# Gate products in eighths around a layer norm's three small matmuls, and the low halves of one weight matrix on VectorE alone

## The chip, the core and the metric

The kernel runs on one core of a Trainium2 chip. A core has TensorE (matrix products, into PSUM), VectorE, ScalarE and GpSimd (work on tiles, each with its own in-order queue), and SyncE, which here issues most loads from memory. The metric is the device time of one execution in microseconds.

## What is computed

One decoder block over 512 tokens of width 1024, float32. The part that the change touches, cut from the reference:

```
u = a * sigmoid(b)                          # gated linear unit
u = causal depthwise conv of width 31 (u) + conv_b
u = silu(layer_norm(u, conv_ln_g, conv_ln_b))
y_conv = u @ w_pw2 + b_pw2
merged = sigmoid(g_attn) * y_attn + sigmoid(g_conv) * y_conv
m = merged @ w_out                          # then x += rms_norm(m); then the squared-ReLU MLP
# layer_norm: mu = mean(x); var = mean((x-mu)^2); (x-mu) * rsqrt(var + eps) * g + b
```

The gate logits g_attn and g_conv are columns of h @ w_in.

## The kernel before

Every large product is made of three in a reduced float32 form: an operand is split in a high half and a low half (the rest), and `mm3` (lines 87 to 91) issues high x high, high x low and low x high. A weight piece is 128 x 512: `wsplit` (line 102) loads it into one of six "raw" tiles from SyncE's queue, casts the high half on ScalarE (line 114) and subtracts on an engine of choice for the low half (line 115). High and low halves of ordinary pieces go into four rotating tiles each, so a cast waits until TensorE has done with the piece four before it.

Work is tiled by blocks of 128 channels over all 512 tokens; a block takes eight steps k of three products of 512 columns, two weight pieces of four steps each. Channels stand on the partitions. `gate_parts` (line 390) is a generator that makes one block of gate logits and yields after each k; `gate` runs it through. Gates 0 to 7 belong to the attention branch; gates 8 to 15 to the convolution branch (names gt8 to gt15 and pg8 to pg15 in the order of instructions, gt and pg in the trace, which leaves numbers out). A gate ends with a multiply on VectorE (line 397) and a sigmoid on ScalarE (line 398) into a tile gB.

The layer norm of the convolution's output has its channels on the partitions, so sums over channels are matmuls with a matrix of ones. There are three small ones: `mub` (the mean, line 581), `st_var` (the variance, line 595, four 128 x 128 weight tiles of squares against one column) and `rsb` (the reciprocal deviation spread over all partitions, line 605). Between mub and st_var stand subtraction of the mean (line 586), squares on ScalarE (588) and sums on GpSimd and VectorE (590 to 593). Between st_var and rsb stand var (598), a power on GpSimd (`rstd_of`, rln, line 148) and four small products with the identity on VectorE (dg, 604). `gates_conv(lo, hi)` runs whole gates: two between mub and st_var, one between st_var and rsb, five after it. After rsb come the norm's scaling and swish (609 to 615), which make the split operand swh and swl.

Then `w_pw2` is multiplied block by block (pyb, line 631; its pieces' low halves are made on GpSimd), each block's result is merged with the gates and the attention branch into m (633, 634) and split into mgh and mgl. In between `load_wout(k)` loads row block k of w_out, with its low half (wol) on VectorE for odd k and on GpSimd for even k. Then `project_out` (pm, line 662) multiplies by w_out.

The order on each engine is set when the program is built: a scheduler places instructions by program order, dependencies and its own estimate of when they are ready. Each engine then runs its list strictly in that order.

Of the kernel before, what the change touches and what calls it, by code (L numbers as in the profile page):

```python
# [23 lines left out]
KD = D // P  # L24
# [9 lines left out]
NC_ = C // P  # L34
# [17 lines left out]
BRIDGE = 4  # L52
SPLIT = 2 * P
TAIL = 2
LN0, LN1, LN2 = 0, 2, 3


@with_exitstack
def decoder_block(ctx: ExitStack, tc: tile.TileContext, a: dict, out: bass.AP):
    nc = tc.nc  # L60
    pe, act, dve, pool, sp = nc.tensor, nc.scalar, nc.vector, nc.gpsimd, nc.sync
# [25 lines left out]
    def mm3(o, lh, ll, rh, rl, first, last):  # L87

        pe.matmul(o, lhsT=lh, rhs=rh, start=first, stop=False)  # L89
        pe.matmul(o, lhsT=lh, rhs=rl, start=False, stop=False)  # L90
        return pe.matmul(o, lhsT=ll, rhs=rh, start=False, stop=last)  # L91
# [10 lines left out]
    def wsplit(src, name, sizes=(512, 512), dst=None, eng=None):  # L102

        parts, off = [], 0
        for p, n in enumerate(sizes):
            raw = rtile(f"{name}_{p}", n)
            sp.dma_start(raw, src[:, off:off + n])
            if dst is None:
                hi = stage.tile([P, 512], F32R, tag="whi", name=f"whi_{name}_{p}", bufs=NSPLIT)[:, :n]
                lo = stage.tile([P, 512], F32R, tag="wlo", name=f"wlo_{name}_{p}", bufs=NSPLIT)[:, :n]  # L110
            else:
                hi, lo = (d[:, off:off + n] for d in dst)
            e = eng or pool
            recent[act] = act.copy(hi, raw)  # L114
            recent[e] = e.tensor_tensor(lo, raw, f32(hi), ALU.subtract)  # L115
            parts.append((off, n, hi, lo))
            off += n

        def cols(c0, n):
            for o, m, hi, lo in parts:  # L120
                if o <= c0 and c0 + n <= o + m:
                    return hi[:, c0 - o:c0 - o + n], lo[:, c0 - o:c0 - o + n]
            raise ValueError(f"columns {c0}:{c0 + n} of {name} lie in two pieces")

        return cols

    def stat(name, n=1, tag="stat", bufs=8):
        return const.tile([P, n], F32, tag=tag, name=name, bufs=bufs)
# [31 lines left out]
    def hsl(x, k, sl):  # L160
        return hT[x][k // 4][:, k % 4, sl]
# [8 lines left out]
    def ps(name):  # L170
        return psum.tile([P, 512], F32, tag="ps", name=name, bufs=3)
# [4 lines left out]
    def tps(name):  # L176
        return psum.tile([P, 512], F32, tag="tp", name=name, bufs=1)
# [29 lines left out]
    with ExitStack() as s1:  # L207
        r1 = open_pool(s1, "r1")
        w0 = []
        for k in range(KD):  # L210
# [5 lines left out]
            hi, lo = (r1.tile([P, Z0], F32R, tag=f"w0{x}", name=f"w0{x}{k}", bufs=8) for x in "hl")  # L216
# [173 lines left out]
    def gate_parts(i, dst):  # L390
        w = wsplit(a["w_zm"][2 * NC_ + i], f"gt{i}")
        pg = ps(f"pg{i}")
        for k in range(KD):
            mm3(pg, *w(k * P, P), hsl(0, k, full), hsl(1, k, full), k == 0, k == KD - 1)
            if k < KD - 1:
                yield
        dve.tensor_tensor(dst, pg, rxs, ALU.mult)
        act.activation(dst, dst, AF.Sigmoid)

    def gate(i, dst):  # L400
        for _ in gate_parts(i, dst):
            pass
# [3 lines left out]
    with ExitStack() as s3:  # L406
# [89 lines left out]
        for n in range(NT * H):  # L496
            h, i = divmod(n, NT)
# [22 lines left out]
    def wtile(name, dt=F32):  # L520
        return r3.tile([P, 2, 512], dt, tag="w", name=name, bufs=14)
# [5 lines left out]
    mA, gB = [], []  # L527
    for i in range(NC_):
# [3 lines left out]
        else:  # L532
            for _ in g0:
                pass
            for pr in range(H // 2):
                hi, lo = wtile(f"ah{pr}", F32R), wtile(f"al{pr}", F32R)
# [15 lines left out]
    for i0 in range(0, NC_, 2):  # L552
        acc = [cvtile(f"cv{i0 + j}") for j in range(2)]
        co = [upool.tile([P, S + 32], F32, tag="u", name=f"c{i0 + j}", bufs=9)[:, :S] for j in range(2)]
        for tap in range(CW):
            for j in range(2):
                i = i0 + j
# [10 lines left out]
            elif i0 + j:  # L568
                (dve if i0 + j == NC_ - 1 else pool).tensor_tensor(csum, csum, co[j], ALU.add)

    def gates_conv(lo, hi):
        for i in range(lo, hi):
            if i % 2 == 0:
                gB.append(wtile(f"gB{i}"))
            gate(NC_ + i, gB[i // 2][:, i % 2, :])

    gates_conv(0, LN0)


    mub = cvtile("mub")  # L580
    pe.matmul(mub, lhsT=ones, rhs=csum, start=True, stop=True)
    gates_conv(LN0, LN1)
    st_var = tps("st_var")
    s2 = []
    for i in range(NC_):
# [7 lines left out]
    dve.tensor_tensor(s2[7], s2[3], s2[7], ALU.add)  # L593
    for t in range(NT):
        pe.matmul(st_var[:, t:t + 1], lhsT=s2[7][:, t * P:(t + 1) * P], rhs=ones[:, 0:1], start=True, stop=True)
    gates_conv(LN1, LN2)
    var = stat("var", NT)
    dve.tensor_scalar(var, st_var[:, 0:NT], 1.0 / C, EPS, ALU.mult, ALU.add)
    rs = rstd_of(var, "rln", NT)
# [2 lines left out]
    for t in range(NT):  # L602
        sl = slice(t * P, (t + 1) * P)
        dve.tensor_scalar(dg[:, sl], ident, rs[:, t:t + 1], None, ALU.mult)
    pe.matmul(rsb, lhsT=ones, rhs=dg, start=True, stop=True)
    gates_conv(LN2, NC_)
    sw = [[r3.tile([P, 4, S], F32R, tag="sw", name=f"sw{x}{g}", bufs=4) for g in range(2)] for x in "hl"]
    for i in range(NC_):
        dve.tensor_tensor(cs[i], cs[i], rsb, ALU.mult)
# [10 lines left out]
    def load_wout(k):  # L620
        hi, lo = (wtile if k < 6 else ratile)(f"woh{k}", F32R), (wtile if k < 6 else ratile)(f"wol{k}", F32R)
        wsplit(a["w_out"][k], f"wout{k}", dst=[x.rearrange("p a b -> p (a b)") for x in (hi, lo)],
               eng=dve if k % 2 else pool)
        wo.append((hi, lo))

    mg = [[hpool.tile([P, 4, S], F32R, tag="h", name=f"mg{x}{g}", bufs=4) for g in range(2)] for x in "hl"]
    for i in range(NC_):
        w = wsplit(a["w_pw2"][i], f"pw{i}")
        py = ps(f"pyb{i}")
        for k in range(NC_):  # L630
            mm3(py, *w(k * P, P), sw[0][k // 4][:, k % 4, :], sw[1][k // 4][:, k % 4, :], k == 0, k == NC_ - 1)
        m_ = stile(f"m{i}")
        dve.scalar_tensor_tensor(m_, py, bpw[:, i:i + 1], gB[i // 2][:, i % 2, :], ALU.add, ALU.mult)
        dve.tensor_tensor(m_, m_, mA[i], ALU.add)
        split_psum(mg[0][i // 4][:, i % 4, :], mg[1][i // 4][:, i % 4, :], m_)
        while len(wo) < min(KD, i + 2):
            load_wout(len(wo))


    while len(wo) < KD:  # L640
        load_wout(len(wo))
# [257 lines left out]
def build(arrays):  # L899
    import concourse.bacc as bacc  # L900

    nc = bacc.Bacc("TRN2", target_bir_lowering=False, num_devices=1, dynamic_dma_scratch_size=8192)
    args = {}
    for n, v in arrays.items():
        args[n] = nc.dram_tensor(f"in_{n}", v.shape, mybir.dt.from_np(v.dtype), kind="ExternalInput").ap()
    o = nc.dram_tensor("out_0", (S, D), F32, kind="ExternalOutput").ap()
    with tile.TileContext(nc) as tc:
        decoder_block(tc, args, o)
    return nc
# [9 lines left out]
```

## Time and profile before

| | us |
|---|---|
| median of 3 runs | 820.9 (820.53 to 821.85) |
| the profiled execution | 821.58 |
| its span | 819.8 |
| TensorE busy | 789.4 (96%) |
| VectorE busy | 631.7 (77%) |
| ScalarE busy | 419.7 (51%) |
| GpSimd busy | 215.6 (26%) |

Busy shares are means over stages with different limits. TensorE's matmuls are pipelined: a row of 0.39 us for a product of 512 columns contains a tail that overlaps the next, and what counts is the distance between starts. The granted clock is a share of TensorE's full 2.4 GHz, so 0.50 is 1.2 GHz. Times of rows are microseconds from the span's start.

### The profile page before, as it was taken

How to read it: one execution, taken by the hardware profiler on the slowest of the kernel's cores; microseconds unless marked ns; L12 is line 12 of the kernel's file. 1: busy time of each engine (PE TensorE's matmuls, PEld its weight loads, DVE VectorE, ACT ScalarE, POOL GpSimd, SP SyncE). 2: the span in 40 equal slices, each digit the busy share in tenths (PEclk: the TensorE clock that was granted, in tenths of full speed). 3: DMA queues.
4: the chain of work that ended last, by engine and by line, in shares of the span. 5: the costliest groups of instructions: out<-in, count | busy, mean ns of one | idle time of the engine just before them, and what ended most of it. 6: DMA issues, size and time to landing. Idle time of an engine off the chain costs nothing. (4 is left out here: it accounts for less than half of the span.)

```text
span 819.8 us, 11002 instructions
## 1 busy us (share of the span) xinstructions
PE 789.4 (96%) x3786; PEld 662.7 (81%) x3786; DVE 631.7 (77%) x1046; ACT 419.7 (51%) x792; POOL 215.6 (26%) x203
## 2 busy tenths in 40 slices
PE   8989999999999999899999999999999999999991
PEld 8977888888887888687877898888888888788881
DVE  5689999999999996587563538676766666798777
ACT  7566876876763323366442314444444344556642
POOL 4244334333534545647640110000000000000003
PEclk9999999999999999899999999999999999999996
DMA  8412121122112223235551014444433434565422
GB/s 269 137 42 91 52 81 53 45 88 71 65 65 90 97 97 113 93 134 171 172 191 39 17 36 154 142 167 142 162 133 129 155 128 146 179 214 204 167 69 102
DMA packets 54344, 96.36 MB, mean 118 GB/s; under 512 B 6288, under 2 KB 11280, under 8 KB 54288
## 3 DMA queue, kind: packets, MB, share of 16 engines
q1 hardware_dynamic: 53856, 94.09, 34.3%
q0 software_dynamic: 432, 1.57, 0.6%
q8 instruction: 30, 0.49, 0.3%
q14 instruction: 26, 0.21, 0.1%
HBM read 93.54 MB, written 2.10 MB: 117 GB/s over the span
## 5 line engine op out<-in xcount | busy, mean ns | idle before, releaser
L562 DVE SCALAR_TENSOR_TENSOR cv<-u,convw,cv 128x512 f32<-128x512 f32 x232 | 161.9, 747 | 0.2
L90 PE MATMUL pf<-h2l,whi_f 128*128 128x512 f32 (+1 forms) x256 | 96.2, 376 | 0.0
L89 PE MATMUL pf<-h2h,whi_f 128*128 128x512 f32 (+1 forms) x256 | 96.2, 376 | 0.0
L91 PE MATMUL pf<-h2h,wlo_f 128*128 128x512 f32 (+1 forms) x256 | 96.0, 376 | 0.0
L115 DVE TENSOR_TENSOR wlo_f<-raw_f,whi_f 128x512 fp32r<-128x512 f32 x60 | 41.1, 691 | 61.1 <-ACT whi_f L114 58.8
L852 POOL TENSOR_TENSOR e<-e,v 128x512 f32<-128x512 f32 x2 | 3.2, 1594 | 321.5 <-DVE e L849 321.5
L114 ACT CAST whi_f<-raw_f 128x512 fp32r<-128x512 f32 x60 | 36.9, 621 | 81.4 <-DMA raw_f<-in_w_ff 42.7
L115 POOL TENSOR_TENSOR wlo_gt<-raw_gt,whi_gt 128x512 fp32r<-128x512 f32 x32 | 43.9, 1373 | 50.5 <-ACT whi_gt L114 50.5
L89 PEld LDWEIGHTS pf<-h2h,whi_f 128*128 128x128 f32 x256 | 48.2, 188 | 8.8
L90 PEld LDWEIGHTS pf<-h2l,whi_f 128*128 128x128 f32 x256 | 48.2, 188 | 8.7
L91 PEld LDWEIGHTS pf<-h2h,wlo_f 128*128 128x128 f32 x256 | 48.2, 188 | 8.7
L89 PE MATMUL pg<-hTh,whi_gt 128*128 128x512 f32 x128 | 51.9, 405 | 0.0
L90 PE MATMUL pg<-hTl,whi_gt 128*128 128x512 f32 x128 | 50.8, 397 | 0.0
L91 PE MATMUL pg<-hTh,wlo_gt 128*128 128x512 f32 x128 | 50.7, 396 | 0.0
L89 PE MATMUL p<-yh,l 128*128 128x512 f32 x128 | 49.7, 390 | 0.0
L90 PE MATMUL p<-yl,l 128*128 128x512 f32 x128 | 49.7, 389 | 0.0
L91 PE MATMUL p<-yh,l 128*128 128x512 f32 x128 | 49.5, 389 | 0.0
L729 ACT CAST yh<-f 128x512 fp32r<-128x512 f32 x48 | 28.1, 619 | 32.8 <-PE p L90 25.2
L730 DVE TENSOR_TENSOR yl<-f,yh 128x512 fp32r<-128x512 f32 x48 | 31.7, 686 | 12.9 <-ACT yh L729 12.9
L114 ACT CAST whi_gt<-raw_gt 128x512 fp32r<-128x512 f32 x32 | 19.8, 618 | 41.3 <-PE pg L90 38.4
L729 ACT CAST xh<-t 128x512 fp32r<-128x512 f32 x48 | 29.8, 621 | 19.5 <-DVE t L754 19.5
L730 DVE TENSOR_TENSOR xl<-t,xh 128x512 fp32r<-128x512 f32 x48 | 31.6, 686 | 0.0
(314 smaller groups left out, 2279.8 us busy)
## 6 DMA issues: line engine op xcount, KB each, us to landing
f<-in_w_ff SPq DMA_DIRECT2D x128, 256.0 KB, 3.0
raw_f<-in_w_ff SPq DMA_DIRECT2D x64, 256.0 KB, 3.1
raw_gt<-in_w_zm SPq DMA_DIRECT2D x32, 256.0 KB, 2.5
raw_gb<-in_w_zm SPq DMA_DIRECT2D x16, 256.0 KB, 2.6
raw_ga<-in_w_zm SPq DMA_DIRECT2D x16, 256.0 KB, 2.6
raw_wo<-in_w_o SPq DMA_DIRECT2D x16, 256.0 KB, 2.6
raw_pw<-in_w_pw SPq DMA_DIRECT2D x16, 256.0 KB, 2.9
raw_wout<-in_w_out SPq DMA_DIRECT2D x16, 256.0 KB, 2.7
```

The costliest lines, as they stand in the source:

```text
L89: pe.matmul(o, lhsT=lh, rhs=rh, start=first, stop=False)
L90: pe.matmul(o, lhsT=lh, rhs=rl, start=False, stop=False)
L91: return pe.matmul(o, lhsT=ll, rhs=rh, start=False, stop=last)
L114: recent[act] = act.copy(hi, raw)
L115: recent[e] = e.tensor_tensor(lo, raw, f32(hi), ALU.subtract)
L562: dve.scalar_tensor_tensor(co[j] if tap == CW - 1 else acc[j], src, convw[:, i, tap:tap + 1], acc[j], ALU.mult, ALU.add)
L729: act.copy(hi, src)
L730: dve.tensor_tensor(lo, src, f32(hi), ALU.subtract)
L852: pool.tensor_tensor(e[:, t, :], e[:, t, :], v, ALU.add)
```

## The change

The three constants that named whole gates become two that count eighths of gates: 21 eighths between mub and st_var (gates 8 and 9 and five eighths of gate 10), five between st_var and rsb (the rest of gate 10 and two eighths of gate 11), the other 38 after rsb. The second call also moves in program order, from ahead of var to behind dg. And w_out's low halves are all made on VectorE.

```
-LN0, LN1, LN2 = 0, 2, 3
+LN1, LN2 = 21, 5
...
-    def gates_conv(lo, hi):
-        for i in range(lo, hi):
+    def gates_conv():
+        for i in range(NC_):
             if i % 2 == 0:
                 gB.append(wtile(f"gB{i}"))
-            gate(NC_ + i, gB[i // 2][:, i % 2, :])
-
-    gates_conv(0, LN0)
+            yield from gate_parts(NC_ + i, gB[i // 2][:, i % 2, :])
+            yield
+
+    gates = gates_conv()
+
+    def run_gates(n):
+
+        for _ in range(n):
+            next(gates, None)
 
 
     mub = cvtile("mub")
     pe.matmul(mub, lhsT=ones, rhs=csum, start=True, stop=True)
-    gates_conv(LN0, LN1)
+    run_gates(LN1)
     st_var = tps("st_var")
...
         pe.matmul(st_var[:, t:t + 1], lhsT=s2[7][:, t * P:(t + 1) * P], rhs=ones[:, 0:1], start=True, stop=True)
-    gates_conv(LN1, LN2)
     var = stat("var", NT)
...
         dve.tensor_scalar(dg[:, sl], ident, rs[:, t:t + 1], None, ALU.mult)
+    run_gates(LN2)
     pe.matmul(rsb, lhsT=ones, rhs=dg, start=True, stop=True)
-    gates_conv(LN2, NC_)
+    run_gates(NC_ * KD)
...
         wsplit(a["w_out"][k], f"wout{k}", dst=[x.rearrange("p a b -> p (a b)") for x in (hi, lo)],
-               eng=dve if k % 2 else pool)
+               eng=dve)
```

How instructions move, at three places. TensorE around st_var, before (pg9 is gate 9's accumulator, pg10 gate 10's):

```order
L90 MATMUL pg9_3602<-hTl1_103,whi_gt9_1_3598 128x512
L91 MATMUL pg9_3602<-hTh1_101,wlo_gt9_1_3599 128x512
L595 MATMUL st_var_3629<-ones_86,s27_3656 128x1 x4
L89 MATMUL pg10_3678<-hTh0_100,whi_gt10_0_3668 128x512
L90 MATMUL pg10_3678<-hTl0_102,whi_gt10_0_3668 128x512
```

and now:

```order
L91 MATMUL pg10_3642<-hTh0_100,wlo_gt10_0_3633 128x512
L89 MATMUL pg10_3642<-hTh1_101,whi_gt10_1_3638 128x512
L90 MATMUL pg10_3642<-hTl1_103,whi_gt10_1_3638 128x512
L91 MATMUL pg10_3642<-hTh1_101,wlo_gt10_1_3639 128x512
L601 MATMUL st_var_3658<-ones_86,s27_3685 128x1 x4
L89 MATMUL pg10_3642<-hTh1_101,whi_gt10_1_3638 128x512
L90 MATMUL pg10_3642<-hTl1_103,whi_gt10_1_3638 128x512
```

Five eighths of gate 10 have moved ahead of st_var.

GpSimd around the power rln, before (wlo_gt11_1 is the low half of gate 11's second weight piece):

```order
L115 TENSOR_TENSOR wlo_gt11_0_3719<-raw_gt11_0_3716,whi_gt11_0_3718 128x512
L115 TENSOR_TENSOR wlo_gt11_1_3725<-raw_gt11_1_3722,whi_gt11_1_3724 128x512
L148 TENSOR_TENSOR rln_3707<-var_3705,mhalf_87 128x4
L115 TENSOR_TENSOR wlo_gt12_0_3759<-raw_gt12_0_3756,whi_gt12_0_3758 128x512
L115 TENSOR_TENSOR wlo_gt12_1_3765<-raw_gt12_1_3762,whi_gt12_1_3764 128x512
```

and now:

```order
L115 TENSOR_TENSOR wlo_gt11_0_3718<-raw_gt11_0_3715,whi_gt11_0_3717 128x512
L115 TENSOR_TENSOR wlo_gt11_1_3724<-raw_gt11_1_3721,whi_gt11_1_3723 128x512
L115 TENSOR_TENSOR wlo_gt12_0_3759<-raw_gt12_0_3756,whi_gt12_0_3758 128x512
L148 TENSOR_TENSOR rln_3696<-var_3694,mhalf_87 128x4
L115 TENSOR_TENSOR wlo_gt12_1_3765<-raw_gt12_1_3762,whi_gt12_1_3764 128x512
```

The power has moved behind the low half of gate 12's first piece.

VectorE at the beginning of the pointwise products, before (swl1 is the last channel's low half; wol1 a low half of w_out's second row block; m0 the first merged block):

```order
L615 TENSOR_TENSOR swl1_3916<-si7_3967,swh1_3914 128x512
L397 TENSOR_TENSOR gB6_3834<-pg14_3847,rxs_266 128x512
L115 TENSOR_TENSOR wol1_4030<-raw_wout1_0_4031,woh1_4029 128x512
L115 TENSOR_TENSOR wol1_4030<-raw_wout1_1_4035,woh1_4029 128x512
L397 TENSOR_TENSOR gB6_3834<-pg15_3886,rxs_266 128x512
L633 SCALAR_TENSOR_TENSOR m0_4014<-pyb0_3989,vecs_90,gB0_3550 128x512
```

and now:

```order
L621 TENSOR_TENSOR swl1_3916<-si7_3967,swh1_3914 128x512
L115 TENSOR_TENSOR wol0_4020<-raw_wout0_0_4021,woh0_4019 128x512
L115 TENSOR_TENSOR wol0_4020<-raw_wout0_1_4025,woh0_4019 128x512
L115 TENSOR_TENSOR wol1_4030<-raw_wout1_0_4031,woh1_4029 128x512
L115 TENSOR_TENSOR wol1_4030<-raw_wout1_1_4035,woh1_4029 128x512
L397 TENSOR_TENSOR gB6_3834<-pg15_3886,rxs_266 128x512
L115 TENSOR_TENSOR wol2_4082<-raw_wout2_0_4083,woh2_4081 128x512
L115 TENSOR_TENSOR wol2_4082<-raw_wout2_1_4087,woh2_4081 128x512
L639 SCALAR_TENSOR_TENSOR m0_4014<-pyb0_3989,vecs_90,gB0_3550 128x512
```

Four low halves have been added ahead of m0, and gate 14's multiply now stands ahead of swl1.

## Rows read from the trace of the kernel before

**Rows 1.** TensorE's waits: tile, releaser, us in total, times, longest.

```profile
PE st_var L595 <- DVE s L593: 3.0, 1, 3.0
PE cta L273 <- DVE cTl L95: 2.2, 1, 2.2
PE pyb L91 <- POOL wlo_pw L115: 2.0, 3, 0.8
PE sc L89 <- ACT knh L94: 1.6, 1, 1.6
...
PE pm L91 <- DVE mgl L95: 0.6, 1, 0.6
```

**Rows 2.** Timeline of TensorE around st_var: start, us, instruction, idle before.

```profile
335.06 0.39 PE L91 MATMUL pg<-hTh,wlo_gt 128*128 128x512 f32 x1
...
338.46 0.39 PE L91 MATMUL pg<-hTh,wlo_gt 128*128 128x512 f32 x1
341.84 1.87 PE L595 MATMUL st_var<-ones,s 128*128 128x1 f32 x8 [2.99 <-DVE s L593]
...
348.41 0.48 PE L91 MATMUL pg<-hTh,wlo_gt 128*128 128x512 f32 x1
...
351.48 1.02 PE L605 MATMUL rsb<-dg,ones 128*128 128x512 f32 x2
```

**Rows 3.** Stretches: length, busy by engine, PEclk, DMA share, GB/s.

```profile
52.00:53.00 1.00, 1.00 (x5) 0.90 (x4) 1.00 (x2) 0.47 (x3) 1.00 (x2) 0.50 0.00 0
...
81.00:82.00 1.00, 0.06 (x1) 0.06 (x1) 0.97 (x2) 0.97 (x3) 0.00 (x0) 1.00 0.03 10
...
344.00:346.00 2.00, 2.00 (x6) 1.52 (x6) 0.88 (x4) 0.00 (x0) 1.02 (x1) 0.50 0.00 0
```

**Rows 4.** The page's VectorE line: busy tenths in 40 slices of 20.5 us.

```profile
DVE  5689999999999996587563538676766666798777
```

**Rows 5.** Timeline of the other engines between the squares and rsb.

```profile
340.15 1.63 DVE L593 TENSOR_TENSOR s<-s,s 128x512 f32<-128x512 f32 x1
...
342.42 0.63 ACT L398 ACTIVATE gB<-gB 128x512 f32<-128x512 f32 x1 [3.14 <-DVE gB L397]
...
343.99 1.04 POOL L148 TENSOR_TENSOR rln<-var,mhalf 128x4 f32<-128x4 f32 x1 [2.75 <-DVE var L598]
...
345.06 0.88 DVE L604 TENSOR_SCALAR dg<-ident,rln 128x128 f32<-128x128 f32 x4 [1.15 <-POOL rln L148]
...
349.39 1.29 POOL L115 TENSOR_TENSOR wlo_gt<-raw_gt,whi_gt 128x512 fp32r<-128x512 f32 x1 [4.37 <-ACT whi_gt L114]
```

**Rows 6.** Timeline of VectorE and GpSimd where a tensor_scalar meets a subtraction.

```profile
356.48 1.52 DVE L612 TENSOR_SCALAR c<-c,vecs 128x512 f32<-128x512 f32 x1
...
356.08 1.63 POOL L115 TENSOR_TENSOR wlo_gt<-raw_gt,whi_gt 128x512 fp32r<-128x512 f32 x1 [2.60 <-ACT whi_gt L114]
```

**Rows 7.** Timeline of TensorE: first pyb product, the first miss, pm's first product.

```profile
379.57 0.39 PE L89 MATMUL pyb<-swh,whi_pw 128*128 128x512 f32 x1
...
388.97 0.50 PE L91 MATMUL pyb<-swh,wlo_pw 128*128 128x512 f32 x1 [0.63 <-POOL wlo_pw L115]
...
426.14 0.39 PE L89 MATMUL pm<-woh,mgh 128*128 128x512 f32 x1
```

**Rows 8.** Timeline of GpSimd ahead of the first two misses.

```profile
387.19 1.73 POOL L115 TENSOR_TENSOR wlo_pw<-raw_pw,whi_pw 128x512 fp32r<-128x512 f32 x1
...
407.28 5.95 POOL L115 TENSOR_TENSOR wol<-raw_wout,woh 128x512 fp32r<-128x512 f32 x4 [1.59 <-ACT woh L114]
```

**Rows 9.** Groups by form, 320 to 440: busy us, mean ns, idle before.

```profile
L115 POOL TENSOR_TENSOR wol<-raw_wout,woh 128x512 fp32r<-128x512 f32 x8 | 11.6, 1469 | 1.9 <-ACT woh L114 1.8
...
L115 DVE TENSOR_TENSOR wol<-raw_wout,woh 128x512 fp32r<-128x512 f32 x8 | 8.6, 1102 | 9.2 <-ACT woh L114 9.1
```

**Rows 10.** Timeline of VectorE: the norm's first scaling and the last low half.

```profile
352.54 1.88 DVE L609 TENSOR_TENSOR c<-c,rsb 128x512 f32<-128x512 f32 x3 [0.17 <-PE rsb L605]
...
377.11 1.37 DVE L615 TENSOR_TENSOR swl<-si,swh 128x512 fp32r<-128x512 f32 x1 [0.35 <-ACT swh L614]
```

## The prediction

> **What bounds the kernel now.** I read the page's busy line first, then TensorE's waits over the whole span, then the timeline at each long wait. TensorE is the bound: the five longest waits that concern us sum to 9.4 us [rows 1] in a span of 819.8. A change pays only if it shortens one of those waits or what hangs on it. Two lie in the stretch that the diff touches: 3.0 us before the variance's column sums (st_var), and 2.0 us in three pieces before the pointwise products (pyb), each for a low half that GpSimd makes. A third, 0.6 us (pm for mgl), follows at once.
>
> The 3.0 us is not the whole price of the first. The last product of gate 9 issues at 338.46, st_var at 341.84 [rows 2]. TensorE, which had been busy until then, runs at 1.2 GHz afterwards: the granted clock is 0.50 in 344 to 346 [rows 3], and the last slow product issues at 348.41 [rows 2]. Those 6.57 us at half clock cost 3.3 us more. The same happened after the 2.2 us wait for cTl, with 0.50 at 52 to 53, but not after the 1.6 us wait for knh, with 1.00 at 81 to 82 [rows 1, 3]. So a wait of 1.6 us has been free of the second cost, one of 2.2 us has not.
>
> **Part 1: eighths.** No instruction is added; eight yields per gate let the two sums stand between eighths. Fifteen products (five eighths) of gate 10 come ahead of st_var, and fifteen (three of gate 10, two of gate 11) between st_var and rsb, where 0 and 24 stood.
>
> - Ahead of st_var. Fifteen products take 335.06 to 338.46 = 3.40 us [rows 2], 0.227 each. TensorE is then free at 338.46 + 0.23 + 3.40 = 342.09. VectorE, whose order up to here is unchanged, ends the sum of squares at 340.15 + 1.63 = 341.78 [rows 5]. The wait is gone with 0.3 us to spare, and with it the fall of the clock. St_var's eight passes took 1.87 us at half clock [rows 2], so about 0.95 at full: 343.05. The next fifteen end at 346.45.
> - What is late next: rsb. It needs var, the power on GpSimd (rln) and the four dg on VectorE. GpSimd's order has changed: the low half of gate 12's first piece now stands ahead of rln. It waits for a cast on ScalarE, which stands behind gate 9's sigmoid, over at 342.42 + 0.63 = 343.05 [rows 5]. A cast of the same 0.6 us ends near 343.65; the low half takes 1.29 [rows 5] to 344.95; rln takes 1.04 [rows 5] to 346.0. Without that row rln could have begun at 343.4, so the new place costs 1.5 us.
> - Then dg. Behind rln stands the low half of gate 12's second piece. Its cast waits for gate 10's last product but one, which ends near 345.0, so it is ready near 345.8, as rln ends. In the trace such VectorE work stands still while GpSimd subtracts: a tensor_scalar that began at 356.48, 0.4 us after a GpSimd subtraction, ended at 358.0, 0.3 us after that subtraction did [rows 6]. I therefore let GpSimd go first: 1.29 more, to 347.3, then dg's 0.88 [rows 5], to 348.2. The bounds are 346.9 (dg first) and 348.2 (behind); I take the latter because the rows lie nearest to it.
> - Sum. Rsb issued at 351.48 [rows 2], after 24 of these products; now at 348.2 after 30. 351.48 - 348.2 + 6 x 0.227 = **4.6 us**; with dg first 5.9 us. The gap at rsb is 348.2 - 346.45 = 1.75 us less a product's tail, near the 1.6 us that left the clock alone.
>
> The Trainium skill, "SBUF — State Buffer", section "Who interferes with whom", says that VectorE and GpSimd share one port pair, held for a whole instruction, and that a tensor_scalar in a two-port mode, or a VectorE operation with two SBUF inputs against a GpSimd one that reads SBUF, blocks until the other is done. By that rule part 1 is worth the 4.6 us; were there no such lock, 5.9. The trace agrees [rows 6].
>
> After rsb the remaining gates run as before, 114 products where 120 stood; TensorE waits nowhere in that stretch [rows 1], since each weight piece is cast a gate or more ahead. The layer norm's chain on VectorE took from 352.54 to 377.11 + 1.37 = 378.48, 25.9 us [rows 10], and ended 1.1 us before the first pyb product at 379.57 [rows 7]. It now starts 6 products (1.4 us) nearer to pyb and has one gate's multiply more in it, so it ends about 1 us after pyb starts. The last channel is needed only at pyb's eighth step, 7 x 3 x 0.227 = 4.8 us in. Cost nothing; 3.8 us of cover.
>
> **Part 2: low halves on VectorE.** GpSimd loses eight subtractions of 1.47 us, 11.8 us; VectorE, which took 1.10 for the same [rows 9], gains 8.8 us, while it was busy five to seven tenths in the slices from 369 to 430 [rows 4]. GpSimd's low half for pyb at 387.19 came directly after two of them, and TensorE missed it by 0.63; four more fill 407.28 to 413.2 ahead of the second miss [rows 7, 8]. The third follows from the second through the raw tile that it frees late. Without them each low half of pyb can start as soon as its cast is done, 2.9 us earlier at the first place and over 1 us at the second. From the first pyb product at 379.57 to the first of pm at 426.14 pass 46.57 us [rows 7]; 192 products of 0.227 are 43.5. So the three misses cost **3.0 us**, more than their idle. Bounds: 0 (every miss returns for its load) and 3.0. I take 3.0: the missing time is under 1 us each and the time freed larger.
>
> The wait for mgl, 0.6 us, comes from VectorE's backlog behind the late low halves of w_out. With the loads earlier it should go: **0.6**, bounds 0 and 0.6. Head of line: six w_out subtractions now stand ahead of the first m on VectorE. M frees a PSUM bank needed two products' rounds (10.9 us) later, so a delay of a few us hides.
>
> **Sum.** 4.6 + 3.0 + 0.6 = 8.2 us. The profiled execution took 821.58 us (its span and 1.8 us around it): 813.4. The median of the runs, 820.9, is 0.7 below it, so I forecast **812.7**. What comes after pm follows TensorE and shifts with it.
>
> **The rivals.**
> - *No lock at dg.* The second piece's cast comes after dg, so rsb issues at 346.9: 5.9 + 3.6 = 9.5, 811.4. For it: the cast beats rln's end by only 0.2 us. Against: [rows 6], and dg is four instructions that can be cut into.
> - *Clock falls at rsb.* The gap is 1.7 us, between 1.6 (kept) and 2.2 (lost) [rows 1, 3]. Price up to the 3.3 us paid before [rows 2]: 812.7 to 816.0, 815 if it falls for most of that.
> - *Pyb still waits.* The cast of a pyb piece stands behind that of a w_out piece whose raw tile now waits for VectorE, which finishes the norm chain 1 us into pyb. Two of the 3.0 us stay and mgl's 0.6 too: 4.6 + 1.0 = 5.6, 815.3. Against: the pieces keep over 1 us of margin by the sum above.
> - *It does not do what it says.* The squares' sum ends 0.3 us before TensorE is free; if GpSimd's subtractions hold it back more, st_var waits again. Even so the wait is under 1 us, so only a fall of the clock with it brings the time near 820.
> - *Slower.* Place: VectorE at m0. If a w_out subtraction ahead of it waits for its load past the start of pyb's fourth round (three banks, 3 x 24 x 0.227 = 16.3 us after pyb's start), TensorE stops; each us beyond costs one, and 3.3 more once the gap passes 2.2. It has to last 6.5 us to eat the 8.2 and pass 0.2% (1.6 us, about what runs of this kernel can tell from none). No wait of that length for VectorE stands in TensorE's list [rows 1].
>
> **How the numbers follow.** Forecast 0.50 (812.0 to 813.4), no lock 0.15, clock 0.13, pyb 0.14, nothing 0.05, slower 0.03. The range reaches from 810.9, the no-lock case with 0.5 of spread, to 815.6, which takes in pyb's case and the half of the clock's with the smaller price: 0.50 + 0.15 + 0.12 + 0.06 = 0.83. Faster by over 0.2%: 0.94; within: 0.03; slower: 0.03.
>
> **What would show it.** St_var with no idle before it, and granted clock 1.00 through 340 to 350. An idle of about 1.7 us before rsb, with a GpSimd subtraction between rln and dg's end. Rsb near 348.2, pyb's first product near 375, its last 43.5 us later without a wait for GpSimd, none for mgl. The forecast is wrong if VectorE's w_out subtractions appear as what TensorE or ScalarE waits for, or if the clock stands at 0.50 after rsb.

## The result, and the profile after

The changed kernel took 817.4 us (median of 6 runs, 816.83 to 819.53) beside 821.38 for the kernel before: 0.9949 of it, with a 95% interval of 0.9931 to 0.9967. Run again beside its variants (a2_after) it took 818.51 beside 822.87, 0.9936 (0.9915 to 0.9958). It is faster, by 4.0 to 4.4 us where 8.2 were forecast, and 817.4 lies outside the range of 810.9 to 815.6.

TensorE's waits over the whole span of the changed kernel: tile, releaser, us in total, times, longest.

```profile
PE cta L273 <- DVE cTl L95: 2.2, 1, 2.2
PE pyb L91 <- POOL wlo_pw L115: 1.6, 3, 0.9
PE sc L89 <- ACT knh L94: 1.6, 1, 1.6
PE p L89 <- ACT xh L735: 1.6, 1, 1.6
PE rsb L611 <- DVE dg L609: 1.3, 1, 1.3
...
PE pm L91 <- DVE mgl L95: 0.6, 1, 0.6
...
PE pyb L89 <- ACT whi_pw L114: 0.3, 1, 0.3
```

Beside [rows 1]: the 3.0 us at st_var are gone and 1.3 at rsb stand in their place, as forecast. But pyb still waits for GpSimd's low halves three times (1.6 us for 2.0) and now once for ScalarE's high half, mgl's 0.6 us stay, and p, at the start of the feed-forward part's second sweep, waits 1.6 us; the kernel before has 0.87 there.

Before the numbers are set side by side, one caution. Up to mub, the first of the norm's small sums, every engine has the same instructions in the same order in all kernels here, yet mub's first product issued between 326.9 and 330.4 us in the thirteen profiled executions that are compared. I take that difference for no effect of a change, so times below are counted from mub. (The profiled execution of e4_gmlp_late, 1320.67 us at a granted clock of 0.558, was in a slow state and is not compared.)

| profiled execution | mub | rsb after mub | pyb after mub | pyb stage (first pyb to first pm product) | first p behind its wait, after the first pm product | end after mub |
|---|---|---|---|---|---|---|
| before | 326.90 | 24.58 | 52.67 | 46.57 | 285.66 | 492.9 |
| after | 328.76 | 21.04 | 47.90 | 46.60 | 286.37 | 488.9 |
| after, second time (a2_after) | 328.60 | 21.03 | 47.88 | 45.88 | 286.39 | 488.2 |

So part 1 gave 52.67 - 47.90 = 4.8 us by the time pyb begins. The pyb stage, which was to give 3.0, gave 0 (0.7 in the second execution), and 0.7 us were given back at p, the first product of the feed-forward part's second sweep. The whole is 4.8 + 0 - 0.7 = 4.1, against 492.9 - 488.9 = 4.0.

The norm stage went as the prediction's steps have it. TensorE around rsb and VectorE's and GpSimd's part of it, in the changed kernel (timeline: start, us, engine, instruction, idle before):

```profile
345.53 1.30 POOL L115 TENSOR_TENSOR wlo_gt<-raw_gt,whi_gt 128x512 fp32r<-128x512 f32 x1 [2.40 <-ACT whi_gt L114]
346.78 1.04 POOL L148 TENSOR_TENSOR rln<-var,mhalf 128x4 f32<-128x4 f32 x1
347.81 1.27 POOL L115 TENSOR_TENSOR wlo_gt<-raw_gt,whi_gt 128x512 fp32r<-128x512 f32 x1
...
347.86 1.89 DVE L609 TENSOR_SCALAR dg<-ident,rln 128x128 f32<-128x128 f32 x4 [2.76 <-POOL rln L148]
...
349.80 1.13 PE L611 MATMUL rsb<-dg,ones 128*128 128x512 f32 x2 [1.34 <-DVE dg L609]
```

Dg took 1.89 us where it took 0.88 [rows 5], and the subtraction that began 0.05 us ahead of it is the reason forecast; e6 and e8 below, without that subtraction, bear it out. The granted clock is 1.00 in 326 to 347 and in 347 to 376; it was 0.50 in 344 to 346 [rows 3].

What failed is in the pyb stage. TensorE's first pyb product and its misses, in the changed kernel:

```profile
376.66 0.39 PE L89 MATMUL pyb<-swh,whi_pw 128*128 128x512 f32 x1
...
382.96 0.50 PE L91 MATMUL pyb<-swh,wlo_pw 128*128 128x512 f32 x1 [0.25 <-POOL wlo_pw L115]
...
410.31 0.50 PE L89 MATMUL pyb<-swh,whi_pw 128*128 128x512 f32 x1 [0.32 <-ACT whi_pw L114]
...
411.93 0.50 PE L91 MATMUL pyb<-swh,wlo_pw 128*128 128x512 f32 x1 [0.88 <-POOL wlo_pw L115]
...
418.15 0.50 PE L91 MATMUL pyb<-swh,wlo_pw 128*128 128x512 f32 x1 [0.47 <-POOL wlo_pw L115]
```

The norm's chain on VectorE, its begin and its end:

```profile
350.97 1.88 DVE L615 TENSOR_TENSOR c<-c,rsb 128x512 f32<-128x512 f32 x3 [0.62 <-PE rsb L611]
...
375.78 1.67 DVE L619 TENSOR_TENSOR si<-si,c 128x512 f32<-128x512 f32 x1
377.37 0.68 DVE L397 TENSOR_TENSOR gB<-pg,rxs 128x512 f32<-128x512 f32 x1
378.14 0.69 DVE L621 TENSOR_TENSOR swl<-si,swh 128x512 fp32r<-128x512 f32 x1
379.25 2.50 DVE L115 TENSOR_TENSOR wol<-raw_wout,woh 128x512 fp32r<-128x512 f32 x4 [0.42 <-ACT woh L114]
```

The chain that took 25.9 us [rows 10] takes 378.83 - 350.97 = 27.9, and ends 2.2 us after pyb's first product, where it ended 1.1 us ahead of it. Behind it on VectorE stand the first subtractions for the output projection's weights, at 2.6 us into pyb. The casts that these need stand behind the chain too, in ScalarE's queue:

```profile
377.48 0.63 ACT L620 CAST swh<-si 128x512 fp32r<-128x512 f32 x1 [2.58 <-DVE si L619]
378.08 0.64 ACT L398 ACTIVATE gB<-gB 128x512 f32<-128x512 f32 x1
378.62 2.17 ACT L114 CAST woh<-raw_wout 128x512 fp32r<-128x512 f32 x4
380.69 0.62 ACT L114 CAST whi_pw<-raw_pw 128x512 fp32r<-128x512 f32 x1
```

The last row is the pw2 piece of the first miss. It was issued at 375.49 and landed 2.6 us later; its cast then waited another 2.6 us, behind the late swh, a gate's sigmoid and four casts of w_out. The later misses come by another road. Each subtraction of w_out frees a raw tile, and SyncE's loads of the same stretch show what follows:

```profile
375.49 1.76 SPq L107 DMA_DIRECT2D raw_pw<-in_w_pw  x2
379.98 0.93 SPq L107 DMA_DIRECT2D raw_wout<-in_w_out  x2
381.18 0.93 SPq L107 DMA_DIRECT2D raw_pw<-in_w_pw  x2
...
385.55 0.80 SPq L107 DMA_DIRECT2D raw_pw<-in_w_pw  x2
...
393.15 2.03 SPq L107 DMA_DIRECT2D raw_pw<-in_w_pw  x2
...
411.90 1.58 SPq L107 DMA_DIRECT2D raw_pw<-in_w_pw  x2
```

The third pair of pw2 pieces is issued at 381.18, 4.5 us into pyb, and the eighth at 411.90, 35.2 us in. Its first low half is ready near 418.1, when TensorE already waits. As I read these rows, the pieces go through six raw tiles one behind the other (load, cast, subtraction, free tile, next load), and a late start is handed on to the end of the stage.

### The profile page after: what moved, and what is told of

It reads as the page before. It is cut to its first block, busy times and chain, and to the rows that moved or that the text cites. A ratio compares the mean times of both kernels' runs of the same rounds, so it can differ in the third digit from the quotient of the medians.

```text
span 817.7 us, 11001 instructions
## 1 busy us (share of the span) xinstructions
PE 788.0 (96%) x3786; PEld 661.8 (81%) x3786; DVE 637.1 (78%) x1054; ACT 419.1 (51%) x792; POOL 203.2 (25%) x195
## 5 line engine op out<-in xcount | busy, mean ns | idle before, releaser
L115 POOL TENSOR_TENSOR wlo_gt<-raw_gt,whi_gt 128x512 fp32r<-128x512 f32 x32 | 43.5, 1359 | 48.7 <-ACT whi_gt L114 48.7
L735 ACT CAST yh<-f 128x512 fp32r<-128x512 f32 x48 | 28.1, 619 | 33.9 <-PE p L90 25.5
```

The costliest lines, as they stand in the source:

```text
L735: act.copy(hi, src)
```

## The experiments

The first theory (T) was: the second part gave nothing, because the loads' chain and not the subtracting engine sets pyb's misses. Its rival (R): the second part works, and part 1's earlier arrival ate it. All ratios below are to the kernel before on the same chip.

### Each part alone: e1_part1_only, e2_part2_only

```
e1, from after:       eng=dve)   ->   eng=dve if k % 2 else pool)
e2, from before:      eng=dve if k % 2 else pool)   ->   eng=dve)
```

> The changed kernel with the low halves of the output projection's weights shared between VectorE and GpSimd again, as before the change: only the handing out by eighths is left. Theory T (the second part gave nothing): the gain of the whole change is the first part's 4.9 us less what the second sweep gives back, so this kernel takes the changed kernel's time within 1 us, 816.4 to 818.4 us beside 821.4 for the kernel before, and its pyb stage (first pyb product to first pm product) is 46 to 47 us. Rival R (the second part is worth up to 3 us and the first part's hurry ate it): with the second part undone the pyb stage grows to 48 to 50 us and the kernel takes 819 to 821 us.

> The kernel before with the low halves of the output projection's weights on VectorE alone: only the second part of the change. Theory T (the misses in pyb are set by the serial chain of loads through the six raw tiles and by VectorE's norm chain, not by who subtracts): time of the kernel before within 1 us, 820.4 to 822.4 us, pyb stage 46 to 47 us as in the kernel before (46.57). Rival R (it works when pyb is not reached earlier): the three misses of 3.0 us and the wait of 0.6 us at pm go, 817.5 to 818.5 us, pyb stage 43 to 44 us.

Measured: part 1 alone 0.9989 (0.9973 to 1.0004), not told apart from the kernel before; part 2 alone 0.9971 (0.9956 to 0.9985). The pyb stage took 50.38 and 45.36 us. Theory T fell; R was right in direction, but its 43 to 44 us for part 2 alone did not come either. Alone, part 2 shortens the stage by 1.2 us; with part 1 in place, taking it out lengthens the stage from 46.6 to 50.4. And part 1 alone, which brings pyb 4.8 us forward, keeps 1.2 us of them to the end in its profiled execution (491.7 after mub). GpSimd and then TensorE, with the low halves shared (e1):

```profile
409.27 5.92 POOL L115 TENSOR_TENSOR wol<-raw_wout,woh 128x512 fp32r<-128x512 f32 x4 [1.70 <-ACT woh L114]
415.15 2.49 POOL L115 TENSOR_TENSOR wlo_pw<-raw_pw,whi_pw 128x512 fp32r<-128x512 f32 x2
```

```profile
416.46 0.80 PE L91 MATMUL pyb<-swh,wlo_pw 128*128 128x512 f32 x1 [1.89 <-POOL wlo_pw L115]
417.05 0.63 PE L89 MATMUL pyb<-swh,whi_pw 128*128 128x512 f32 x1
417.48 0.63 PE L90 MATMUL pyb<-swl,whi_pw 128*128 128x512 f32 x1
```

This is the row of before at 407.28 [rows 8] over again: four subtractions of w_out ahead of the one that TensorE wants, now at the cost of 1.89 us, with the products behind it 0.43 us apart instead of 0.23. So what the second part was meant for is real. Whether the two parts together (0.9949, 0.9936) give more than the sum of each alone, the intervals do not tell; counted from mub, in single executions, both give 4.0 and 4.7 us, and each alone 1.2 and 0.9. What was still open is why the stage takes 3 us more than its 43.5 with both.

### Which link holds the loads up: e3_wout_order, e4b_gmlp_late

Blocks 4 and 5 of w_out go to tiles that come free only with the third and fifth gated sum. In e3 they come last; in e4b the load of g_mlp, 512 KB that GpSimd issues at 382.86 in the changed kernel, 6.2 us into pyb, is to come later. The expectation says 15 us; in the trace it was issued 33.9 us into pyb, 27.6 us later after mub.

```
e3:  load_wout in the order 0 1 2 3 6 7 4 5
e4b: in pyb's loop, at i == 6:  late = recent[pool].ins
     with tc.issue_after(late):
         gmlp = gain("g_mlp", a["norm_mlp_pre"], D)
```

> The changed kernel with the blocks of the output projection's weights loaded in the order 0 1 2 3 6 7 4 5: blocks 6 and 7 go to tiles that are free, 4 and 5 to tiles that come free only with the third and fifth gated sum, so that blocks 4 and 5 no longer sit in four of the six raw tiles while they wait. Theory T (raw tiles held by blocks 4 and 5 make the load chain serial, a hop of about 5.3 us for each piece): the misses of 0.3, 0.9 and 0.5 us in the second half of pyb go, the first of 0.25 stays, time 815.3 to 816.3 us. Rival (the chain of loads is bound by transfer time or by VectorE's queue, whoever holds the tiles): misses of 1 us or more stay and the time is 817 to 818 us.

> The changed kernel with the load of g_mlp 15 us later, again, beside the changed kernel on the same chip. Theory C (g_mlp's 512 KB among the weight pieces make piece pw3 take 5.5 us, and later hops inherit it): pw3 lands 2 us earlier, misses of pyb shrink from 1.9 us to at most 1 us in sum, 1 us faster than the changed kernel. Theory T (the order in which the raw tiles come free sets the hops): the same time within 0.4 us, misses still 1.5 us or more.

Measured: e3 0.9935 (0.9914 to 0.9957), no different from the changed kernel. Its misses moved from 410 to 418 us to 394 to 402 (0.33, 0.69 and 0.28 us, with 0.25 at 383 as before), and the stage took 46.2 us. The tiles held by blocks 4 and 5 decide where the delay shows, not how large it is.

E4b took 0.9952 (0.9935 to 0.9968), not faster either. The same kernel had run before on e1's chip as e4_gmlp_late, with 0.9948 (0.9933 to 0.9963), 818.43 us, where 815.3 to 816.3 were expected by theory C. In e4b's trace, however, the pieces did what theory C expects: the fifth pair of pw2 is issued 14.0 us into pyb instead of 16.5, only the first miss (0.28), the one by ScalarE's queue, is left, and the stage takes 44.3 us. It lost them again directly behind it:

```profile
427.81 0.50 PE L89 MATMUL pm<-woh,mgh 128*128 128x512 f32 x1 [1.39 <-ACT mgh L94]
...
429.14 0.50 PE L91 MATMUL pm<-woh,mgl 128*128 128x512 f32 x1 [0.61 <-DVE mgl L95]
```

and in its stretches (length, busy of TensorE, granted clock, DMA share, GB/s) the clock falls behind that pair of waits:

```profile
420.00:430.00 10.00, 8.00 (x35) 1.00 0.64 208
430.00:440.00 10.00, 10.00 (x39) 0.83 0.09 29
```

So the transfers' length is one link of the chain: the fourth pair, which lands 5.5 to 5.7 us after its issue in the changed kernel, lands after 3.4 to 3.8 in e4b. Taking time out of it there uncovers the last block's tail: sum, high half, low half, all behind the first weights of the feed-forward part. The moved load may add to that wait, which was not tried: e7 and e9 below, with a stage of 43.5 us, wait 0.7 and 0.3 us for mgh there.

### The norm chain on VectorE: e5_affine_act, e6_gate_lows_dve

Two ways to have that chain end earlier: e5 takes work off VectorE, e6 gives it more work but takes GpSimd out of its way.

```
e5:  -  dve.tensor_scalar(cs[i], cs[i], lng[...], lnb[...], ALU.mult, ALU.add)
     +  act.activation(cs[i], cs[i], AF.Identity, scale=lng[...], bias=lnb[...])
e6:  -  w = wsplit(a["w_zm"][2 * NC_ + i], f"gt{i}")
     +  w = wsplit(a["w_zm"][2 * NC_ + i], f"gt{i}", eng=dve if i >= 12 else None)
```

> The changed kernel with the norm's affine step (scale and shift of each of the 8 blocks, 0.54 us each on VectorE) on ScalarE. Theory V (the pyb stage of the changed kernel waits because VectorE's norm chain, 27.9 us long, ends 2.2 us after pyb has begun, and the casts on ScalarE and the loads behind it start late): VectorE sheds 8 times 0.54 us, 4.3 us, and more where a step stood against GpSimd; the chain ends at least 3 us earlier, the first miss goes and the stage takes 45 to 45.5 us instead of 46.6; 1.0 to 1.5 us faster than the changed kernel. Theory L (the loads set the misses: transfers of 5 us while several are in flight, and the raw tiles behind them): the chain ends earlier, the stage still takes 46 to 46.6 us, time within 0.5 us of the changed kernel.

> The changed kernel with the low halves of the last four gates' weights (eight subtractions of 128x512) on VectorE instead of GpSimd. Theory K (while GpSimd subtracts, VectorE's operations of the norm stage take 1.1 us longer each, as dg did with 1.89 us for 0.88): dg takes 0.9 us, rsb's wait shrinks from 1.34 to at most 0.4 us, and the norm chain is no longer than 27.9 us although it has eight operations of 0.68 us more, since eight long ones become short. Rival (the long operations have another cause, such as waits inside them): dg stays at 1.9 us, the chain grows by 8 times 0.68, 5.4 us, pyb starts late and the time is 1 to 5 us longer than the changed kernel.

Measured: e5 0.9913 (0.9890 to 0.9935), e6 0.9895 (0.9874 to 0.9916), 814.79 us: both faster than the changed kernel's 0.9936 beside them, by about 2 and 3.7 us in the medians. The stages take 43.6 and 43.5 us, and TensorE's list has no wait at pyb left in either. That speaks for theories V and K and against L. The lock is plainest in e6. Its dg with rln just ahead and no subtraction beside it:

```profile
347.54 0.88 DVE L609 TENSOR_SCALAR dg<-ident,rln 128x128 f32<-128x128 f32 x4 [1.15 <-POOL rln L148]
```

and the chain's product si, two SBUF operands, in all eight blocks (count: shortest, median, longest ns; first and last start), in the kernel before, in the changed kernel and in e6:

```profile
L613 DVE TENSOR_TENSOR si<-si,c x8: 676/930/1772, 355.3 to 375.3; 128x512 f32<-128x512 f32 x8
```

```profile
L619 DVE TENSOR_TENSOR si<-si,c x8: 679/1464/1776, 353.8 to 375.8; 128x512 f32<-128x512 f32 x8
```

```profile
L619 DVE TENSOR_TENSOR si<-si,c x8: 677/685/689, 352.5 to 374.1; 128x512 f32<-128x512 f32 x8
```

The multiplication by rsb, which reads one operand from PSUM, has a longest of 0.69 us in all three. With eight operations of 0.68 us more between rsb and its end (six low halves of gates and two of w_out), e6's chain is 376.55 - 349.63 = 26.9 us long, 1.0 less than without them. Rsb no longer waits and comes 19.56 us after mub instead of 21.04.

E5's gain was larger than theory V had it: the chain ended 3.7 us earlier after mub than in the changed kernel, 1.5 us ahead of pyb, and all misses went, not the first alone.

### Parting the steps: e7_both, e8_gate12_only, e9_no_part1, e10_no_part2

```
e7:  e5 and e6 together
e8:  e6 with  eng=dve if i == 12 else None
e9:  e2 (before with part 2) and e6's line
e10: e1 (after without part 2) and e6's line
```

> The changed kernel with both aids: low halves of the last four gates' weights on VectorE, and the norm's affine step on ScalarE. Each alone took all misses out of pyb (stage 43.5 us), so theory V expects little more than with the gates' low halves alone: the same 0.9895 of the kernel before within 0.001, and no wait at rsb. Rival: the wait at the start of the second sweep, 1.99 us there, grows by whatever is gained ahead of it, since loads end it: the same time by another road, with a wait over 2 us.

> The changed kernel with only gate 12's two low halves on VectorE: parts the wait at rsb from the misses in pyb. Theory K (GpSimd's subtraction made dg long): dg 0.9 us, no wait at rsb, rsb 1.4 us earlier after mub than in the changed kernel. Then for pyb: theory V (the rest of the norm chain is still long by GpSimd's other six subtractions) expects a stage of 45 to 46.5 us with two to four misses, since pyb too begins 1.4 us earlier; 0.9920 to 0.9945 of the kernel before. Rival (the start at rsb alone freed the chain): stage 43.5 us, 0.9895.

> The kernel before with the second part of the change and with the last four gates' low halves on VectorE, the gates' order as before. Theory V: the wait of 3.0 us at st_var and the half clock behind it stay, the pyb stage shrinks from 46.6 to 43.5 to 44 us, 2.6 to 3.1 us faster than the kernel before, 0.9962 to 0.9968 of it. Rival (the norm chain mattered only because the first part brought pyb forward): stage as with the second part alone, 45.4 us, 0.997 to 0.9985.

> The changed kernel with the last four gates' low halves on VectorE, but the output projection's low halves shared with GpSimd again, as before the change. It asks whether the second part is still needed once the norm chain is short. Theory V: GpSimd is idle through the norm stage and early with its share, but a wout piece that waits for its transfer still stands ahead of pw2 pieces on GpSimd: one or two misses of 0.5 to 1.9 us, stage 45 to 47.5 us, 0.992 to 0.9945 of the kernel before. Rival: no misses, 43.5 us, 0.9895, and the second part is not needed.

All kernels in one table. Times in the last four columns count from pyb's first product, in the profiled execution; "pieces by GpSimd" says that part of w_out's subtractions stand in GpSimd's queue.

| kernel | ratio to before | norm chain ends | first w_out subtraction | eighth pair of pw2 issued | pyb stage |
|---|---|---|---|---|---|
| before (pieces by GpSimd) | 1 | -1.1 | 0.0 | 34.9 | 46.6 |
| e2, part 2 alone | 0.9971 | -1.1 | -0.6 | 33.4 | 45.4 |
| e1, part 1 alone (pieces by GpSimd) | 0.9989 | +2.2 | +2.7 | 38.2 | 50.4 |
| after, two executions | 0.9949, 0.9936 | +2.2 | +2.6 | 35.2, 34.7 | 46.6, 45.9 |
| e8, gate 12 | 0.9938 | +2.2 | +2.6 | 35.9 | 48.1 |
| e3, w_out order | 0.9935 | +2.2 | +2.6 | 31.8 | 46.2 |
| e4b, g_mlp late | 0.9952 | +2.2 | +2.6 | 32.7 | 44.3 |
| e5, affine on ScalarE | 0.9913 | -1.5 | -1.6 | 32.6 | 43.6 |
| e6, gates' low halves | 0.9895 | +1.3 | -1.8 | 32.1 | 43.5 |
| e7, both | 0.9895 | -2.7 | -2.6 | 32.9 | 43.5 |
| e9, e6 without part 1 | 0.9960 | +0.5 | -3.2 | 32.3 | 43.5 |
| e10, e6 without part 2 (pieces by GpSimd) | 0.9939 | +2.9 | -3.4 | 36.1 | 47.3 |

E8 settles what e6 alone could not: rsb came 19.58 us after mub, as early as in e6, with dg at four times 0.28 us, but the chain still ended 2.2 us into pyb and the stage took 48.1 us, longer than expected, since the clock fell in it (last section). So the early rsb alone does not free the stage; the rival is out. E9 shows the same from the other side: without part 1, and with the chain's end 0.5 us into pyb, no miss is left. The end of the chain is therefore not itself what decides. The column beside it goes with the stage: with all of w_out's subtractions on VectorE, the stage is 43.5 or 43.6 us where the first of them begins at least 1.6 us ahead of pyb, 45.4 at -0.6 (e2), and 45.9 to 48.1 at +2.6; e4b, with shorter transfers, is the one exception. In e6 and e9 that subtraction stands ahead of the last norm steps. No run moved that subtraction alone: e6, e7 and e9 also issue the second pair of pw2 earlier, 3.8 to 6.1 us ahead of pyb for 1.2 in the changed kernel, and only e5, with 2.0, leaves that nearly as it was. That the delay works through the raw tiles and the loads is read from the rows of the loads; it was not tried by itself. The eighth pair's time alone does not tell the stage, since e3 issues it earliest, by its other order, and has 46.2 us. E10 has the first subtraction early too, but half of the pieces on GpSimd, and misses 0.78, 1.84 and 0.22 us: part 2 is needed also when w_out is begun early.

E7 gained nothing measurable over e6, as theory V expected, and its rival's wait of over 2 us at p did not come: p waited 1.3 us. In its place stand waits of 0.7 and 0.6 us at pm for the last block's halves, as in e4b. E6 and e7 beat both the kernel before and the changed one.

## Why the prediction was wrong

- **Part 1, 4.6 us: right.** Rsb was put at 348.2 us. Less the 1.86 us by which mub was later it came at 347.94, with the order, the locked dg and the full clock that the steps gave. Pyb began 4.8 us earlier after mub. The rival without a lock is refuted by dg's row, and its price was about right: e8 and e6, where the lock is gone, have rsb 1.5 us earlier; 1.3 were reckoned. The rival by which the clock falls at rsb did not occur, the wait being 1.34 us.
- **"Cost nothing; 3.8 us of cover": the step that failed.** Two things in it. The chain was to end 1 us into pyb by counting one gate's multiply more; it ended 2.2 us in. GpSimd's subtractions of the gates' weights, whose lock the same text had used for dg, stretch si too, and more than before the change: 1.46 us in the median, where the kernel before has 0.93 and e6, without them, 0.69. And the cover was counted for one customer only. For the chain's own last piece it held: TensorE waits nowhere for swl. The other customers are w_out's subtractions, which stand behind the chain on VectorE and hold the raw tiles that pw2's loads need. These moved from 0.6 us ahead of pyb (e2) to 2.6 behind it, and the eighth pair's load from 33.4 to 35.2. E2, where the chain ends 1.1 us ahead of pyb, still has a stage of 45.4, so a chain that had ended as reckoned, with those subtractions behind it, would hardly have left the stage free. Part 1 brought TensorE forward by 4.8 us and the chain's end by 1.5.
- **Part 2, 3.0 us: measured 0 (0.7 the second time).** Its working treated part 2 by itself, from the gaps of the kernel before, where pyb came 4.8 us later. On that ground it is real but smaller, 1.2 us of stage (e2). Behind part 1 it is worth 3.8 us of stage, against e1, but what it removes there is a loss that part 1 brings along (3.7 us of idle, and a granted clock of 0.72 in 416 to 422 of e1). The reckoning of a miss (2.03 us idle in three, 3.0 lost) did hold: with no miss the stage takes 43.5 or 43.6 us, in e5, e6, e7 and e9.
- **mgl, 0.6 us: measured 0.** It was put down to late subtractions of w_out. The wait is as long in e7 and e9, where pyb misses nothing. In the changed kernel the last sum (m, L639) begins at 425.31 us and its low half only at 428.56; between them stand first pieces of the feed-forward part, which are early and not late. The order was the same before the change (f1l at 430.20, mgl at 431.42 there); no run took those pieces out:

```profile
425.31 0.74 DVE L639 SCALAR_TENSOR_TENSOR m<-pyb,vecs,gB 128x512 f32<-128x512 f32 x1
425.98 0.68 DVE L115 TENSOR_TENSOR wlo_f<-raw_f,whi_f 128x512 fp32r<-128x512 f32 x1
426.57 0.68 DVE L640 TENSOR_TENSOR m<-m,mA 128x512 f32<-128x512 f32 x1
427.35 1.29 DVE L115 TENSOR_TENSOR f1l<-raw_f,f1h 128x512 fp32r<-128x512 f32 x2
428.56 0.68 DVE L95 TENSOR_TENSOR mgl<-m,mgh 128x512 fp32r<-128x512 f32 x1
```

- **"What comes after pm follows TensorE": 0.7 us short.** p waited 1.60 and 1.58 us in two executions of the changed kernel and 0.87 before. ScalarE waits there for a transfer of w_ff2 ahead of the cast. Over all kernels that wait lies between 0.87 (before) and 1.99 us (e6). The three that reach it last, 382.5 to 384.0 us after mub (e1, e2, before), wait 0.87 to 1.04; the others, at 374.4 to 380.2, wait 1.00 to 1.99, in no order (e10 at 378.4 waits 1.00, e8 at 378.8 waits 1.80). So some of what is gained ahead of it can be lost there; what sets how much stays open.
- **The rivals.** "Pyb still waits" named the mechanism: the cast of a pw2 piece behind a w_out piece whose raw tile waits for VectorE. It was given 0.14 and priced as two of the 3.0 us and mgl's 0.6. All of the 3.0 stayed. With 3.0 and 0.6 out, the sum is 4.6, 816.3 by its own scale; the 0.7 at p bring it to 817.0, beside 817.4 measured. The argument against it, "over 1 us of margin", rested on the cover above.

The 8.2 us were there to be had. E6, which gives GpSimd's share of the norm stage to VectorE, took 0.9895 of the kernel before, 8.1 us less in the medians.

## What to carry to other kernels

When TensorE is brought forward, list every piece of work that stands behind the late chain on its engine, not only what TensorE itself reads from it: here the loads, through the tiles that the queued subtractions hold. A gain measured on a gap of the old program is not the gain in the new one, if another part of the same change moves who arrives first; each such term should be worked out again at the new times. Where a lock between two engines is found at one place, look at every place where the same two meet; giving the slower engine's work to the other made the other's chain shorter in two kernels of four, and longer by far less than the work in the other two.

## What was not expected of the hardware

**More operations, a chain hardly longer or even shorter.** Eight subtractions more inside the norm chain on VectorE left that chain 1.0 us shorter (e6 beside the changed kernel), since si fell from 1.46 to 0.69 us in the median; six more left it 1.2 shorter in e7 beside e5. It is no rule: nine more made it 1.2 us longer in e9 beside e2 (27.2 for 26.0), and seven more 0.7 longer in e10 beside e1, though each subtraction takes 0.68 us. The Trainium skill, "SBUF — State Buffer", section "Who interferes with whom", has it that a VectorE instruction with two SBUF inputs contends with a GpSimd one that reads SBUF, and one with a single SBUF input outside the two-port modes does not. The rows agree in both halves: si was stretched up to 1.78 us, while the multiplication with rsb from PSUM was never over 0.69.

**The clock does not go by the length of one wait alone.** In e8 it fell behind waits of 0.83 and 0.88 us, in e10 it stayed full behind 0.78 and 1.84 (TensorE's stretches, columns as above; e8 first):

```profile
408.00:412.00 4.00, 2.44 (x7) 0.86 0.60 181
412.00:418.00 6.00, 6.00 (x23) 0.81 0.45 148
```

```profile
408.00:412.00 4.00, 1.76 (x6) 1.00 0.59 176
412.00:418.00 6.00, 5.78 (x26) 1.00 0.57 188
```

It fell also behind 1.89 us (e1, pyb) and 1.99 (e6, at p: 0.73 in 706 to 712), and stayed at 1.00 behind 1.60 (the changed kernel, at p). E8's stage of 48.1 us holds 1.95 us of idle, and some of the rest is this. A share between 0.50 (1.2 GHz) and 1.00 (2.4 GHz) is the mean of a stretch that holds both levels; in e6 it is 0.50 in 706 to 708 and 0.84 in 708 to 712. The prediction's reading, that 1.6 us are free and 2.2 are not, is too simple: e8's two waits are shorter in sum than e10's, and shorter each than the 1.60 that was free. What else counts was not tried.
